# The FFN's output projection as seven Strassen products in chunks of K, on one Trainium2 core

## The chip, the cores and the metric

The program runs on one core of a Trainium2 chip. The metric is the device time of one execution in microseconds (us); the kernel before takes 2804.18 us (median of 3 runs, 2803.85 to 2805.12). Engines are named as in the profile: PE is TensorE (PEld its weight loads), DVE is VectorE, ACT is ScalarE, POOL is GpSimd, SP is the engine that issues all DMAs here.

## What is computed

A two-layer encoder on x of 1024 tokens by 1024 features, all in float32. Layer 0 mixes tokens by gated linear attention, layer 1 by differential attention. The change touches what follows the mixer in each layer:

```
h = h + mix
g, u = split(rms_norm(h, norm_ffn[i]) @ ffn_w_in[i])       # 1024 -> 2 x 2816
h = h + (silu(g) * u) @ ffn_w_out[i]                       # 2816 -> 1024: the output projection
gate = sigmoid(rms_norm(h, ple_norm[i]) @ ple_w_gate[i])   # 1024 -> 1024: the embedding gate
h = h + gate * (p[i] @ ple_w_proj[i])
```

## The kernel before

**Precision by three products.** Every float32 operand is split by `hi_lo` (line 119) into a rounded part (hi, a ScalarE copy to fp32r) and the rest (lo, a subtraction on VectorE, or on GpSimd where the call says so). `mm3` (line 154) then issues three matmuls, hi x lo, lo x hi and hi x hi (lines 156 to 158), into one PSUM accumulation. So a 128x128 by 128x512 block product costs three matmuls, one ScalarE copy per operand tile and one subtraction per operand tile.

**The FFN** is `ffn` (line 833 on), called once per layer. Its first part already uses seven Strassen products: K is 1024 (two halves of four blocks), and 22 units `u` (11 pairs `jp` of a gate unit and an up unit, 256 columns each) run seven products `(u, p)` each, of 12 matmuls. `prepare` splits weights five products ahead; `evac` adds the products in SBUF; in the up unit's `evac`, GpSimd multiplies into the tiles `sil` (L963), and one DMA per tile writes them to the scratch tensor `a_dram` (L964). The activations stand there transposed: 22 blocks of 128 features by 1024 tokens, even tokens' tiles and odd tokens' tiles side by side.

**The output projection** is the second part: `steps` is 2 halves of the tokens (s) by 22 blocks of K (j). `load_o` loads 128 rows of `ffn_w_out` (512 KB, tile `wr`) and, for each second block, 2 x 256 KB of activations (tile `ar`), four steps ahead. `split_o` splits both, two steps ahead. `out_step` issues 4 token tiles x 2 column halves x 3 matmuls = 24 matmuls into eight PSUM banks that stay open over all 22 blocks, and adds them to `out_h` (tiles `f0h`, reloaded by `load_h` from the scratch copy `h_mid`, four per half) at the half's end with VectorE (L1038).

```
for n in range(2):
    mm3(st["acc"][r][n], both(a, ALL, c), both(w, ALL, sl(n, 512)), j == 0, j == NJ - 1)
```

Beside it `next_pool`, which is `ple_weights`, loads and splits the embedding gate's weights (eight 512 KB tiles `pw_raw`, lo part on GpSimd, 128x1024 each) into a pool of its own. `early` prepares the first gate tile. Then class `Ple` runs the gates tile by tile, 48 matmuls each.

**What sets the order.** PE, DVE, ACT and POOL run their instructions in the order in which the program is written (`manual_schedule`). SP's order is set by the scheduler. All DMAs go out on one queue.

Of the kernel before, what the change touches and what calls it, by code (L numbers as in the profile page):

```python
# [18 lines left out]
P = 128  # L19
S = 1024  # L20
D = 1024
# [43 lines left out]
def kernel(  # L65
# [88 lines left out]
    def mm3(ps, lhs, rhs, start, stop):  # L154
        (lh, ll), (rh, rl) = lhs, rhs
        nc.tensor.matmul(ps, lh, rl, start=start, stop=False)  # L156
        nc.tensor.matmul(ps, ll, rh, start=False, stop=False)  # L157
        nc.tensor.matmul(ps, lh, rh, start=False, stop=stop)  # L158
# [671 lines left out]

    def ffn(layer, hs, tiles, g, hx_pools, bufs, next_pool, early):
# [3 lines left out]
        a_dram = dram.tile([NJ, P, 2, 512], F32, name=f"a_dram{layer}")  # L835
# [100 lines left out]
        def evac(u, p):  # L936
# [23 lines left out]
            else:  # L960
# [3 lines left out]
                nc.sync.dma_start(a_dram[2 * jp + i], sil)  # L964
# [27 lines left out]
        steps = [(s, j) for s in range(2) for j in range(NJ)]  # L992

        def load_o(q):
            s, j = steps[q]
            st["wr", q] = r = rawt(f"f{layer}_{q}wr")
            nc.sync.dma_start(r, w_out[sl(j), :])
            if j % 2 == 0:
                a = rawt(f"f{layer}_{q}ar", [2, 512])
                for i in range(2):  # L1000
                    nc.sync.dma_start(a[:, i, :].rearrange("p (h c) -> p h c", c=256), a_dram[j + i, :, :, sl(s, 256)])
                    st["ar", q + i] = a[:, i, :]

        def split_o(q):
            if q < 2:
                w = [pw.tile([P, D], F32R, tag="w", name=f"f{layer}_{q}wo{i}") for i in range(2)]
                a = pw.tile([P, 2, 512], F32R, tag="w", name=f"f{layer}_{q}ao")
                a = [a[:, i, :] for i in range(2)]
            else:
                if q == 2:  # L1010
                    st["W"] = [block_t(hx_pools[i % len(hx_pools)], f"f{layer}W{i}", bufs) for i in range(2)]
                    st["A"] = block_t(hx_pools[0], f"f{layer}A", bufs)
                i = q % 4
                w = [st["W"][i // 2][:, 2 * (i % 2) + z, :] for z in range(2)]
                a = [st["A"][:, i, sl(z, 512)] for z in range(2)]
            hi_lo(st.pop(("ar", q)), *a)
            hi_lo(st.pop(("wr", q)), *w)
            st["o", q] = (w, a)

        out_h = {}  # L1020
        ORDER = (2, 3, 0, 1)

        def out_step(q):
            s, j = steps[q]
            w, a = st.pop(("o", q))
            if j == 0:
                full = [ptA(f"f{layer}o{s}{i}") for i in range(2)]
                single = [[ptB(f"f{layer}o{s}{i}{n}") for n in range(2)] for i in (2, 3)]
                st["acc"] = [[full[i][:, n, :] for n in range(2)] for i in range(2)] + single
            for i, r in enumerate(ORDER):  # L1030
                if q == len(steps) - 1:
                    early(i, out_h)
                c = sl((r % 2) * 2 + r // 2)
                for n in range(2):
                    mm3(st["acc"][r][n], both(a, ALL, c), both(w, ALL, sl(n, 512)), j == 0, j == NJ - 1)
                for n in range(2 * (j == NJ - 1)):
                    h = out_h[4 * s + r][:, sl(n, 512)]
                    nc.vector.tensor_tensor(h, h, st["acc"][r][n], ALU.add)  # L1038

        def load_h(s):  # L1040
            for r in range(4):
                t = 4 * s + r
                out_h[t] = ht(f"f{layer}h{t}")
                nc.sync.dma_start(out_h[t], h_mid[sl(t), :])

        with tc.manual_schedule(engines={E.PE, E.DVE, E.Activation, E.Pool}):
# [32 lines left out]
            for z in seq:  # L1079
# [6 lines left out]
                else:  # L1086
                    while ready < min(n + (4 if n < 6 else 5), len(prods)):
                        prepare(ready)
                        ready += 1
                    if n == len(prods) - 3:  # L1090
                        for q in range(2):
                            load_o(q)
                        split_o(0)
                    prod(*z)
# [8 lines left out]
            mid.clear()  # L1103
            pool.release()
            later = next_pool()
            split_o(1)
            for q in range(2, 4):
                load_o(q)
            for q in range(len(steps)):
                if q + 2 < len(steps):  # L1110
                    split_o(q + 2)
                if q + 4 < len(steps):
                    load_o(q + 4)
                if 2 <= q < NJ - 4:
                    next(later, None)
                if q % NJ == NJ - 4:
                    load_h(q // NJ)
                if q == len(steps) - 2:
                    early(-1, out_h)
                out_step(q)  # L1120
# [3 lines left out]
    def ple_weights(layer):  # L1124
        pool = open_pool(f"plew{layer}")
        blk = [block_t(pool, f"pg{layer}{i}", 4) for i in range(4)]
        wgt = []

        def load():
            raw = {}  # L1130
            for i in range(KT + 1):
                if i < KT:
                    raw[i] = ht(f"pw{layer}{i}_raw")
                    nc.sync.dma_start(raw[i], ple_w_gate[layer][sl(i), :])
# [5 lines left out]
        return (pool, wgt), load()  # L1140

    class Ple:
# [38 lines left out]
        def nsq(self, t):  # L1181
            nm = f"nd{t}"
            junk = (pw if t == NT - 1 else praw).tile([P, D], F32, tag="w" if t == NT - 1 else "raw", name=nm + "sq")
            ss = tiny.tile([P, 1], F32, tag="ss", name=nm + "ss")
            nc.scalar.activation(junk, self.hs[t], AF.Square, accum_out=ss)
            self.st["nx", t] = self.hs[t] if 4 <= t < NT - 1 else junk, rstd_of(ss, 1, 1.0 / D, nm + "r")
# [4 lines left out]
        def ntr(self, t, hx):  # L1191
            transpose_t(self.st.pop(("nx", t))[0], *hx_t(hx, t), f"nd{t}")


    class Values:
# [16 lines left out]
        def blocks(self, hx, between):  # L1212
            for b in range(4):
                for half in range(2):
                    ps = ptA(f"dv{b}{half}").rearrange("p a (b f) -> p (a b) f", f=256)
                    for i in range(4):
# [11 lines left out]
                        if i < 3:  # L1228
# [3 lines left out]
                    nc.sync.dma_start(self.dram[half * 512:(half + 1) * 512, sl(b, 256)]  # L1232
                                      .rearrange("(k p) f -> p k f", p=P), v)
                    yield

    def diff(hx, hx_pools, h_dram, val, between):
# [387 lines left out]
    for layer in range(2):  # L1624
# [5 lines left out]
        def ple_pool():  # L1630
            (ple["pool"], wgt), gen = ple_weights(layer)
# [125 lines left out]
```

## Time and profile before

| | |
|---|---|
| time, median of 3 runs | 2804.18 us |
| the profiled execution: time, span | 2805.42 us, 2803.6 us |
| PE busy | 2742.5 us (98%) |
| POOL, DVE, ACT busy | 43%, 56%, 46% |
| first part of the FFN, layer 0 | 530 to 957 us of the span |
| output projection, layer 0 and layer 1 | 957 to 1198 us, 2465 to 2705 us |
| granted TensorE clock, mean | 0.998 |

Of an engine's row, busy time is the union of its instructions' spans; a matmul's span is longer than the distance to the next one, since matmuls are pipelined. A wait is read as the idle time before an instruction with what ended it.

### The profile page before, as it was taken

The page shows a single profiled execution, that of the slowest core. Times are in us where ns is not written, and L with a number is a line of the kernel's source. Part 1 is how long each engine was busy: PE and PEld are TensorE (multiplying, and loading weights), DVE is VectorE, ACT ScalarE, POOL GpSimd, SP SyncE. Part 2 cuts the span into 40 slices and gives each one's busy share as a digit, 9 for nine tenths or more (in the row PEclk, how much of TensorE's full clock was granted, in tenths as well). Part 3 has the DMA queues.
Part 4 walks back from the last instruction along what each step waited for, and adds up shares of the span by engine and source line. Part 5 has one row for each costly group of instructions (what it writes and reads, how often), then busy time and mean ns, then how long its engine had stood idle before and what let it go on. Part 6 is the DMA issues. An engine that isn't in the chain of part 4 may idle for free.

```text
span 2803.6 us, 40481 instructions
## 1 busy us (share of the span) xinstructions
PE 2742.5 (98%) x15272; PEld 2373.3 (85%) x15272; DVE 1571.3 (56%) x2390; ACT 1297.1 (46%) x2723; POOL 1204.1 (43%) x1364
## 2 busy tenths in 40 slices
PE   8999999999999999999999999989999999999999
PEld 7899988788888888889988999978878888888887
DVE  5677765654444534354258889886574444444333
ACT  5776663433333332233258878885343323342222
POOL 2243431365555420010578888873165555530000
PEclk9999999999999999999999999999999999999999
DMA  4122255222222564333221111136222222374422
GB/s 123 42 65 61 76 195 196 76 91 91 75 76 90 198 208 143 99 98 112 67 59 43 41 39 42 32 99 214 78 75 91 83 68 90 106 263 142 150 68 83
DMA packets 199956, 283.59 MB, mean 101 GB/s; under 512 B 14545, under 2 KB 158929, under 8 KB 199761
## 3 DMA queue, kind: packets, MB, share of 16 engines
q1 hardware_dynamic: 199760, 281.00, 31.2%
q8 instruction: 121, 1.98, 0.3%
q14 instruction: 75, 0.61, 0.1%
HBM read 215.95 MB, written 65.01 MB: 100 GB/s over the span
## 4 chain that ended last, share of the span: by engine, by line
PE 83%; DVE 7%; POOL 4%; ACT 3%; issue 2%; DMA 1%; SPq 0%; POOLq 0%; DVEq 0%; ACTq 0%
PE f1o L158 3%; PE f0o L156 3%; PE f0o L157 3%; PE f1o L156 3%; PE f1o L157 3%; PE f0o L158 3%; PE dp L156 2%; PE dp L158 2%; PE dp L157 2%; PE dv L156 1%; PE dv L158 1%; PE dv L157 1%; PE do L158 1%; PE do L156 1%; PE do L157 1%
## 5 line engine op out<-in xcount | busy, mean ns | idle before, releaser
L156 PE MATMUL dp<-dw,hxd 128*128 128x256 f32 x512 | 149.0, 291 | 2.0 <-DVE da17dt L1349 0.3
L158 PE MATMUL dp<-dw,hxd 128*128 128x256 f32 x512 | 144.9, 283 | 0.0
L157 PE MATMUL dp<-dw,hxd 128*128 128x256 f32 x512 | 144.7, 283 | 0.0
L156 PE MATMUL f1o<-f1W,f1A 128*128 128x512 f32 x336 | 130.8, 389 | 0.0
L156 PE MATMUL f0o<-f0W,f0A 128*128 128x512 f32 x336 | 130.8, 389 | 0.0
L158 PE MATMUL f0o<-f0W,f0A 128*128 128x512 f32 x336 | 130.7, 389 | 0.0
L158 PE MATMUL f1o<-f1W,f1A 128*128 128x512 f32 x336 | 130.7, 389 | 0.0
L157 PE MATMUL f0o<-f0W,f0A 128*128 128x512 f32 x336 | 130.7, 389 | 0.0
L157 PE MATMUL f1o<-f1W,f1A 128*128 128x512 f32 x336 | 130.7, 389 | 0.0
L156 PEld LDWEIGHTS dp<-dw,hxd 128*128 128x128 f32 x512 | 98.1, 192 | 3.5 <-DVE da17dt L1349 0.6
L157 PEld LDWEIGHTS dp<-dw,hxd 128*128 128x128 f32 x512 | 98.1, 192 | 0.1
L158 PEld LDWEIGHTS dp<-dw,hxd 128*128 128x128 f32 x512 | 97.9, 191 | 0.0
L158 PEld LDWEIGHTS f0o<-f0W,f0A 128*128 128x128 f32 x336 | 63.1, 188 | 13.2
L157 PEld LDWEIGHTS f1o<-f1W,f1A 128*128 128x128 f32 x336 | 63.1, 188 | 13.1
L158 PEld LDWEIGHTS f1o<-f1W,f1A 128*128 128x128 f32 x336 | 63.1, 188 | 13.1
L156 PEld LDWEIGHTS f0o<-f0W,f0A 128*128 128x128 f32 x336 | 63.1, 188 | 13.1
L156 PEld LDWEIGHTS f1o<-f1W,f1A 128*128 128x128 f32 x336 | 63.1, 188 | 12.9
L157 PEld LDWEIGHTS f0o<-f0W,f0A 128*128 128x128 f32 x336 | 63.1, 188 | 12.9
L156 PE MATMUL dv<-dwv,hxd 128*128 128x256 f32 x256 | 73.0, 285 | 0.0
L158 PE MATMUL dv<-dwv,hxd 128*128 128x256 f32 x256 | 72.4, 283 | 0.0
L157 PE MATMUL dv<-dwv,hxd 128*128 128x256 f32 x256 | 72.4, 283 | 0.0
L162 POOL TENSOR_SCALAR pn10r<-pn10ss 128x1 f32<-128x1 f32 x1 | 0.2, 191 | 166.3 <-ACT pn10xn L1152 166.3
(4446 smaller groups left out, 10008.0 us busy)
## 6 DMA issues: line engine op xcount, KB each, us to landing
pw_raw<-in_ple_w_gate_dram SPq DMA_DIRECT2D x16, 512.0 KB, 6.4
dqk_raw<-in_diff_w_in_dram SPq DMA_DIRECT2D x32, 256.0 KB, 3.7
x<-in_x_dram SPq DMA_DIRECT2D x8, 512.0 KB, 6.0
wv_raw<-in_gla_w_in_dram SPq DMA_DIRECT2D x8, 512.0 KB, 4.2
wr_raw<-in_gla_w_in_dram SPq DMA_DIRECT2D x8, 512.0 KB, 3.9
o_dram<-o SPq DMA_DIRECT2D x32, 128.0 KB, 1.8
r_dram<-r SPq DMA_DIRECT2D x16, 256.0 KB, 2.2
gwo_raw<-in_gla_w_out_dram SPq DMA_DIRECT2D x8, 512.0 KB, 3.6
```

The source lines that it names most:

```text
L156: nc.tensor.matmul(ps, lh, rl, start=start, stop=False)
L157: nc.tensor.matmul(ps, ll, rh, start=False, stop=False)
L158: nc.tensor.matmul(ps, lh, rh, start=False, stop=stop)
L162: nc.gpsimd.tensor_scalar(r, ss, scale, EPS, ALU.mult, ALU.add)
```

## The change

**The second product by Strassen as well.** K = 2816 is 22 blocks; blocks are paired into 11 pairs (`jp`): the even blocks are one half of K, the odd ones the other. Even and odd token tiles are the halves of the rows, columns 0 to 511 and 512 to 1023 the halves of the columns. For each pair there are seven left factors and seven right factors.

The left factors are made in the first part, by `sums_o`: after the up unit's multiplications GpSimd does four more 128x512 additions or subtractions per pair, and the seven factors (256 KB each) are written to `a_dram`, now `[8, 11, 128, 512]`. The right factors are made in the second part: `load_b` loads the rows of `ffn_w_out` once (tiles `b1` for even blocks, `b2` for odd ones), and `split_o` has GpSimd subtract 128x512 halves, four per pair, into tile `t` and back into `b1`; each subtraction is issued behind the split that reads the value before.

**Chunks.** The 11 pairs run in chunks of 4, 4 and 3; in a chunk the products come as 1, 5, 6, 3, 7, 2, 4 (in the last one 4 before 2), and each product runs over the chunk's pairs. That gives 28 + 28 + 21 = 77 steps of 12 matmuls (four token tiles x three), where 44 steps of 24 were. A PSUM group X (four banks) takes products 1, 6, 7, 4 one on top of the other, group Y takes 5, 3 and then 2. After a product's last step its running sum is added to four half tiles of `out_h`: after products 2, 3 and 4 by VectorE from PSUM; after 1, 5, 6 and 7 ScalarE copies PSUM to SBUF and GpSimd adds.

```diff
+        chunks = ((0, 4), (4, 4), (8, 3))
+        osteps = [(g, p, j) for g, (_, c) in enumerate(chunks)
+                  for p in ((1, 5, 6, 3, 7, 4, 2) if g == len(chunks) - 1 else (1, 5, 6, 3, 7, 2, 4)) for j in range(c)]
...
+        def load_ar(n):
+            g, p, j = osteps[n]
+            nc.sync.dma_start(half("ar", n % 4), a_dram[p, chunks[g][0] + j])
+
+        def split_o(n):
+            g, p, j = osteps[n]
+            b = lambda q: b_of(q, j)
+            sub = lambda dst, x, y: nc.gpsimd.tensor_tensor(dst, x, y, ALU.subtract)
+            st["o", n] = pair = [pw.tile([P, 2, 512], F32R, tag="w", name=f"f{layer}o{n}{z}") for z in "ab"]
+            for src, z in ((half("ar", n % 4), pair[0]), (b(p), pair[1])):
+                hi_lo(src, z[:, 0, :], z[:, 1, :])
+
+            if p == 1:
+                sub(b(5), b(7), b(1))
+            elif p == 5:
+                sub(b(6), b(3), b(5))
+            elif p == 6:
+                sub(b(4), b(2), b(6))
+            elif p == 3:
+                sub(b(7), b(3), b(7))
...
+            for r in range(4):
+                mm3(acc[r], (a[:, 0, sl(r)], a[:, 1, sl(r)]), (b[:, 0, :], b[:, 1, :]), j == 0 and p in (1, 5, 2), last,
+                    skip_group_check=True)
+            if not last:
+                return
+
+            for r in range(4):
+                h = {1: (1, 0), 2: (1, 0), 5: (0, 1), 7: (0, 1), 6: (1, 1), 3: (1, 1), 4: (0, 0)}[p]
+                h = out_h[2 * r + h[0]][:, sl(h[1], 512)]
+                if p in (2, 3, 4):
+                    nc.vector.tensor_tensor(h, h, acc[r], ALU.add)
+                else:
+                    st["u"] = u = (st.get("u", -1) + 1) % 8
+                    u = half(("t", "ar")[u // 4], 4 + u % 4)
+                    nc.scalar.copy(u, acc[r])
+                    nc.gpsimd.tensor_tensor(h, h, u, ALU.add)
...
             mid.clear()
+            load_h()
+            later = next_pool()
+            for n, (g, p, j) in enumerate(osteps):
+                if n + 4 < len(osteps):
+                    load_ar(n + 4)
+                if n + 2 < len(osteps):
+                    split_o(n + 2)
...
+                if n >= 8 and n % 4 == 0:
+                    next(later, None)
+                out_step(n)
```

Step n is PE's n-th group of 12 matmuls; its two operands (`a`, `b`) are split while step n-2 runs. The tiles of a split come from a pool of six, so a split can begin when PE has finished the step three before it. `load_ar` has four places. All eight tiles of `out_h` are loaded at once at the start of the second part.

**Even tiles first.** Product 4 ends the even token tiles before product 2 ends the odd ones, so the gates now run over tiles 0, 2, 4, 6, 1, 3, 5, 7 (`TILES`), and what reads their order downstream is renumbered (`PLACE`). The gate's weights go to the pools that the FFN's first part has left, their raw tiles to `praw`.

**How SP's order changes, layer 0.** The names: `f_10sil`, `f_10o` are pair 10's factors, `f0h` the tiles of `out_h`, `f0ar` the left factors' four places, `f0b` are `b1` and `b2`. Before, around the last writes of the first part:

```order
L1001 DMA f_2ar<-a_dram_5944 128x2x256 x2
L964 DMA a_dram_5944<-f_10sil_9495 128x1024
L997 DMA f_3wr<-in_ffn_w_out_dram 128x1024
L964 DMA a_dram_5944<-f_10sil_9496 128x1024
L997 DMA f_4wr<-in_ffn_w_out_dram 128x1024
L1001 DMA f_4ar<-a_dram_5944 128x2x256 x2
L997 DMA f_5wr<-in_ffn_w_out_dram 128x1024
L997 DMA f_6wr<-in_ffn_w_out_dram 128x1024
```

Now, at the same place:

```order
L975 DMA a_dram_5944<-f_10sil_9605 128x512
L1031 DMA f0ar<-a_dram_5944 128x512 x2
L975 DMA a_dram_5944<-f_10sil_9606 128x512 x2
L979 DMA a_dram_5944<-f_10o 128x512 x2
L979 DMA a_dram_5944<-f_10sil_9605 128x512
L979 DMA a_dram_5944<-f_10o_9771 128x512
L1080 DMA f0h_9783<-h_mid_5943 128x1024
...
L1080 DMA f0h_9797<-h_mid_5943 128x1024
L1031 DMA f0ar<-a_dram_5944 128x512 x4
L1183 DMA pw_raw<-in_ple_w_gate_dram 128x1024
```

Left factors 0 to 5 are issued ahead; those of steps 6 to 9 stand behind pair 10's seven writes and all eight `f0h` loads.

**POOL in the second part, layer 0.** Before, it had eight subtractions for the gate's weights and nothing else until the first gate tile:

```order
L963 TENSOR_TENSOR f_10sil_9495<-f_10sil_9495,f0cr 128x512 x2
L963 TENSOR_TENSOR f_10sil_9496<-f_10sil_9496,f0cr 128x512 x2
L121 TENSOR_TENSOR pg_9651<-pw_raw,pg_9650 128x1024 x4
L121 TENSOR_TENSOR pg_9653<-pw_raw,pg_9652 128x1024 x4
L162 TENSOR_SCALAR pn00r<-pn00ss 128x1
```

Now, the stretch of chunk 1 (steps 30 to 35 and what they release; L1036 makes right factors, L1075 adds to `out_h`):

```order
L1036 TENSOR_TENSOR f0t<-f0b_9680,f0t 128x512 x2
L1075 TENSOR_TENSOR f0h_9785<-f0h_9785,f0t 128x512
L1075 TENSOR_TENSOR f0h_9789<-f0h_9789,f0t 128x512
L1075 TENSOR_TENSOR f0h_9793<-f0h_9793,f0t 128x512
L1075 TENSOR_TENSOR f0h_9797<-f0h_9797,f0t 128x512
L1036 TENSOR_TENSOR f0t<-f0b_9680,f0t 128x512
L121 TENSOR_TENSOR pg_9802<-pw_raw,pg_9801 128x1024
L1036 TENSOR_TENSOR f0t<-f0b_9680,f0t 128x512 x3
L1075 TENSOR_TENSOR f0h_9783<-f0h_9783,f0ar 128x512
```

Per layer POOL's second part holds 44 right-factor subtractions and 48 additions (128x512) beside the eight gate subtractions (128x1024).

## Rows read from the trace of the kernel before

**Rows 1.** The page: busy time of the engines; a group of the costliest ones.
```profile
PE 2742.5 (98%) x15272; PEld 2373.3 (85%) x15272; DVE 1571.3 (56%) x2390; ACT 1297.1 (46%) x2723; POOL 1204.1 (43%) x1364
...
L156 PE MATMUL f0o<-f0W,f0A 128*128 128x512 f32 x336 | 130.8, 389 | 0.0
```

**Rows 2.** Tile f0o: duration ns min/median/max, first and last start.
```profile
L156 PE MATMUL f0o<-f_0wo,f_0ao x8: 389/389/389, 957.4 to 962.1; 128*128 128x512 f32 x8
```

**Rows 3.** Tile pl00g, the first gate.
```profile
L156 PE MATMUL pl00g<-pg,pn x16: 389/389/473, 1197.6 to 1208.8; 128*128 128x512 f32 x16
```

**Rows 4.** Windows: PE, PEld, DVE, ACT, POOL busy (instructions), PEclk, DMA share, GB/s.
```profile
530.00:957.40 427.40, 423.46 (x1858) 348.21 (x1857) 207.16 (x279) 139.53 (x243) 241.90 (x180) 1.00 0.27 90
957.40:1197.60 240.20, 240.20 (x1065) 199.01 (x1064) 97.09 (x105) 75.23 (x96) 26.22 (x14) 1.00 0.50 160
```

**Rows 5.** Groups by form in the output projection: busy, mean ns, idle before.
```profile
L121 DVE TENSOR_TENSOR f0A<-f_14ar,f0A 128x512 fp32r<-128x512 f32 x2 | 1.4, 692 | 6.5 <-ACT f0A L120 6.5
...
L120 ACT CAST f0A<-f_14ar 128x512 fp32r<-128x512 f32 x2 | 1.2, 624 | 7.7 <-PE f0o L158 7.7
```

**Rows 6.** Timeline of POOL in the first part, then at its end: start, length.
```profile
691.79 2.54 POOL L963 TENSOR_TENSOR f_3sil<-f_3sil,f0cr 128x512 f32<-128x512 f32 x2 [1.05 <-DVE f0cr L948]
694.29 1.30 POOL L121 TENSOR_TENSOR f_8w<-f_8s,f_8w 128x512 fp32r<-128x512 f32 x1
...
958.35 3.90 POOL L963 TENSOR_TENSOR f_10sil<-f_10sil,f0cr 128x512 f32<-128x512 f32 x2 [1.43 <-DVE f0cr L948]
973.23 2.49 POOL L121 TENSOR_TENSOR pg<-pw_raw,pg 128x1024 fp32r<-128x1024 f32 x1 [10.98 <-ACT pg L120]
```

**Rows 7.** Timeline of DVE where both DVE and POOL have work.
```profile
2050.71 1.77 DVE L121 TENSOR_TENSOR f1T<-nf17sq,f1T 128x512 fp32r<-128x512 f32 x1
2052.40 1.78 DVE L121 TENSOR_TENSOR f_0w<-f_0a,f_0w 128x512 fp32r<-128x512 f32 x1
2054.10 1.77 DVE L121 TENSOR_TENSOR f1T<-doh,f1T 128x512 fp32r<-128x512 f32 x1
2055.80 1.78 DVE L121 TENSOR_TENSOR f_1w<-f_1s,f_1w 128x512 fp32r<-128x512 f32 x1
2057.50 0.68 DVE L944 TENSOR_TENSOR f1cr<-f1cr,f_1ps 128x512 f32<-128x512 f32 x1
```

**Rows 8.** Timeline of POOL in the same stretch.
```profile
2053.59 1.74 POOL L917 TENSOR_TENSOR f_1a<-f_1a 128x512 f32<-128x512 f32 x1
2055.29 1.74 POOL L921 TENSOR_TENSOR f_1a<-f_1a,f_1s 128x512 f32<-128x512 f32 x1
2056.99 1.74 POOL L121 TENSOR_TENSOR f1T<-doh,f1T 128x512 fp32r<-128x512 f32 x1
```

**Rows 9.** Timeline of PE: the first part's product (8, 5).
```profile
701.93 0.39 PE L157 MATMUL f_8ps<-f0T,f_8w 128*128 128x512 f32 x1
```

**Rows 10.** Timeline of SP: the last write of the first part.
```profile
962.28 0.33 SPq L964 DMA_DIRECT2D a_dram<-f_10sil  x1
```

**Rows 11.** DMA issues: KB each, median us from issue to landing.
```profile
f0h<-h_mid SPq DMA_DIRECT2D x8, 512.0 KB, 4.3
...
f_0wr<-in_ffn_w_out_dram SPq DMA_DIRECT2D x2, 512.0 KB, 4.4
f_0ar<-a_dram SPq DMA_DIRECT2D x4, 256.0 KB, 3.2
```

**Rows 12.** Windows in two bursts of loads; columns as in Rows 4.
```profile
940.00:944.00 4.00, 4.00 (x19) 3.31 (x18) 0.69 (x1) 2.55 (x5) 2.34 (x2) 1.00 0.99 380
968.00:972.00 4.00, 4.00 (x19) 3.30 (x18) 2.52 (x3) 2.94 (x4) 0.00 (x0) 1.00 0.99 383
```

**Rows 13.** Windows around a wait of PE; columns as in Rows 4.
```profile
555.40:558.00 2.60, 0.57 (x2) 0.19 (x1) 2.11 (x3) 2.60 (x6) 2.60 (x3) 1.00 0.06 21
558.00:561.50 3.50, 3.50 (x8) 2.79 (x9) 2.78 (x3) 0.66 (x3) 3.33 (x2) 0.51 0.00 0
```

**Rows 14.** Timeline of PE in that second window.
```profile
559.43 0.63 PE L157 MATMUL f_0ps<-f0T,f_0w 128*128 128x512 f32 x1
559.86 0.63 PE L158 MATMUL f_0ps<-f0T,f_0w 128*128 128x512 f32 x1
```

More of the change, by code (lines that the diff above doesn't have):

```diff
@@ L989, in prepare @@
                 sums_a2(u)
[L992 to L1018, printed above, removed]
@@ L1020, in ffn @@
-        out_h = {}
[L1021 to L1038, printed above, removed]
@@ new lines, in out_step @@
+        def out_step(n):
+            g, p, j = osteps[n]
+            last = j == chunks[g][1] - 1
+            if j == 0 and p == 1:
+                st["X"] = [z[:, i, :] for z in [ptA(f"f{layer}o{g}x{i}") for i in range(2)] for i in range(2)]
+                st["Y"] = [ptB(f"f{layer}o{g}y{i}") for i in range(4)]
+            if j == 0 and p == 2 and g == len(chunks) - 1:
+                st["Y"] = [z[:, i, :] for z in [ptA(f"f{layer}o{g}z{i}") for i in range(2)] for i in range(2)]
+            acc = st["X" if p in (1, 6, 7, 4) else "Y"]
+            a, b = st.pop(("o", n))
+            for r in range(4):
+                mm3(acc[r], (a[:, 0, sl(r)], a[:, 1, sl(r)]), (b[:, 0, :], b[:, 1, :]), j == 0 and p in (1, 5, 2), last,
[12 more added lines that the diff above has]
+                    nc.gpsimd.tensor_tensor(h, h, u, ALU.add)
@@ L1043, in load_h @@
+        def load_h():
+            for t in range(NT):
                 out_h[t] = ht(f"f{layer}h{t}")
@@ L1103, in ffn, with ple_weights @@
             mid.clear()
-            pool.release()
[L1105 to L1120, printed above, removed]
+            load_h()
[5 more added lines that the diff above has]
+                    split_o(n + 2)
+                    if osteps[n + 2][1:] == (2, 0) and g + 1 < len(chunks):
+                        load_b(g + 1, 0)
+                    if osteps[n + 2][1:] == (4, 0) and g + 1 < len(chunks):
+                        load_b(g + 1, 1)
+                if n >= 8 and n % 4 == 0:
+                    next(later, None)
+                out_step(n)
+                if g == len(chunks) - 1 and (p, j) == (4, chunks[g][1] - 1):
+                    early(0, out_h)
+                if g == len(chunks) - 1 and (p, j) == (2, 1):
+                    early(1, out_h)
+            for _ in later:
+                pass
+            pool.release()
         return [out_h[t] for t in range(NT)]
-    def ple_weights(layer):
-        pool = open_pool(f"plew{layer}")
-        blk = [block_t(pool, f"pg{layer}{i}", 4) for i in range(4)]
+    TILES = (0, 2, 4, 6, 1, 3, 5, 7)
+    PLACE = {t: i for i, t in enumerate(TILES)}
+    def ple_weights(layer, pools, bufs):
+        blk = [block_t(pools[i % len(pools)], f"pg{layer}{i}", bufs) for i in range(4)]
         wgt = []
@@ L1139, in load @@
                 yield
-        return (pool, wgt), load()
+        return wgt, load()
     class Ple:
```

129 lines of the change are left out of this document (77 added, 52 removed).

## The prediction, made before the changed kernel was run

> **What bounds the kernel now.** I read the page first: PE is busy in 98% of the span [rows 1], so PE is the limit, and other engines matter where they make PE wait. The page gives 389 ns for a matmul of the output projection. That is a length, not a price, since matmuls overlap. So I read the stage itself: its first matmul starts at 957.4 us [rows 2], the first gate's at 1197.6 [rows 3]. In between stand 44 steps of 24 = 1056 matmuls: 240.2 / 1056 = **0.2275 us each**, with no idle time, since the window shows PE busy in all of its 240.2 us [rows 4]. The same window says how empty the other engines are there: DVE 97 us, ACT 75, POOL 26. In the first part of the FFN POOL is busy 242 of 427 us [rows 4].
>
> Then I looked for what new work would collide with. Where DVE and POOL both have a queue, subtractions that POOL does alone in 2.54 / 2 = 1.27 us [rows 6] and DVE in 0.69 [rows 5] come strictly in turn: DVE starts at 2050.71, 2052.40, 2054.10, 2055.80, POOL at 2053.59, 2055.29, 2056.99, both 1.70 apart [rows 7, 8]. So a pair, one of each, costs **1.70 us**, nearly the sum of the two. Only DVE's addition that reads PSUM takes its 0.68 beside a running POOL instruction [rows 7]. The reader is to see that for subtractions from SBUF the two engines are one resource.
>
> **What is removed.** Per layer 77 steps of 12 = 924 matmuls stand where 1056 were: 132 x 0.2275 = **-30.0 us** per layer. A step takes 12 x 0.2275 = 2.73 us of PE. By the 389 ns of the page it would be -51; the 0.2275 decides, since it is what the stage's end moves by.
>
> **What costs nothing.** ACT: two copies of 0.62 [rows 5] a step, 1.25 of 2.73, with bursts of four PSUM copies per product; a split runs two steps ahead, which covers it. DMA: some 40 MB in about 215 us, 190 GB/s against 380 in a burst [rows 12]; what it costs is the order, below. The four new POOL instructions per pair in the first part stand ahead of the split of the next unit's product 5. In the trace POOL is done with the multiplications at 694.33 and has 1.30 for that split [rows 6]: 694.33 + 4 x 1.27 + 1.30 = 700.7, with a DVE turn (0.43) in between 701.1; PE reads it at 701.93 [rows 9]. Hidden, with 0.8 to spare; if the cover is gone, every further DVE turn costs 0.43 at 10 places a layer. The order of the gates moves no work.
>
> **The load of `out_h`: a wait.** Count from PE's start of step 0. Before, POOL ended the last multiplication at 962.25 [rows 6], and SP issued the last write at 962.28 [rows 10], 4.9 us after that start. Now four subtractions follow on POOL, at 1.27 to 1.70 each, so the last of seven writes goes out at 10.0 to 11.7; I take 11. SP issues in order, so the eight loads of `out_h`, 512 KB each, come behind it, and the left factor of step 6 behind all eight. The first load lands 4.3 us after its issue [rows 11]; in a burst the queue moves 380 GB/s [rows 12], 1.37 us per load; 7 x 1.37 = 9.6, and 0.7 for the 256 KB of the factor. With 0.3 for issuing, 11 + 0.3 + 4.3 + 9.6 + 0.7 = 25.9; two ACT copies and the last DVE subtraction (0.62 + 0.62 + 0.69) give 27.8. PE is due at step 6 after 6 x 2.73 = 16.4. **+11.4 us** per layer. Bounds: 9 (POOL undisturbed, 3.2 us to the first landing as for the 256 KB loads), 13 (POOL always in turn, slower burst). POOL sits behind the same loads with its first additions, so what is late next is its queue.
>
> After such a wait PE's clock can be low: following a window in which PE was busy for 0.57 of 2.60 us the granted clock is 0.51 for 3.5 us, the 1.2 GHz level [rows 13], and matmuls start 0.43 us apart [rows 14]. Eight matmuls there cost 8 x (0.43 - 0.2275) = **+1.6 us**; ends 0 and, for two such stretches, 3.2.
>
> **DVE and POOL in turns: the largest unknown.** Each step needs two DVE subtractions. POOL gets 44 subtractions for right factors, 48 additions into `out_h` and the 8 long ones for the gates, 2.49 us each [rows 6], which is 1.2 more than a short one: a pair with a long one costs 2.90. As long as POOL has a backlog, two pairs = 3.40 us go by per step, and PE, which needs 2.73, is held to that. The backlog comes in a lump, since a chunk's sums for products 5, 6, 4 and 7 and the additions of products 1, 5 and 6 all fall between the ends of products 1 and 3:
> - chunk 1 (steps 28 to 55): 22 short and 3 long in a row = 22 x 1.70 + 3 x 2.90 = 46.1 us for 12.5 steps, for which PE needs 34.1. The splits are 1.1 us ahead when it begins: +10.9;
> - chunk 0: part of the backlog drains in the wait above; 14 short and 2 long = 29.6 for 8 steps, 21.8, lead 2.2: +5.6;
> - chunk 2 (three pairs): 19 short = 32.3 for 9.5 steps, 25.9, lead 1.8: +4.6.
>
> **+21.1 us** per layer. From below: if DVE always came first, PE would wait only for the chunk's last right factors, some 8.8 in chunk 1 (32.4 us of POOL and 14.3 of DVE in the 37.9 until the last is due) and 3 in the others: 12. From above: the pair costs the whole of both lengths, 1.30 + 0.69 = 1.99: the three lumps come to 10.2 + 18.1 + 10.1 = 38. I take 1.70, the one number of rows in which the same two shapes meet.
>
> The Trainium skill, SBUF — State Buffer, Who interferes with whom, says that a VectorE instruction with two SBUF inputs contends with GpSimd's reads, and that whoever issues first has the shared ports for the whole instruction. Taken by the profile's lengths that is the 1.99 and a time of about 2849; rows 7 and 8 show 1.70, so the measurement decides.
>
> **Chunk ends.** Group X of the next chunk (of product 2, in the last) waits for DVE's additions of product 4, which stand behind a split: the second of them (2 x 0.68) ends about 0.4 late, three times: **+1.2**; ends 0 and 2.
>
> **The sum** per layer: -30.0 + 11.4 + 1.6 + 21.1 + 1.2 = +5.3; two layers **+10.6**. The profiled execution took 2805.4 and would take 2816.0; it was 1.2 above the median of 2804.2, so I give **2815**.
>
> **Rivals.**
> 1. *The turns do not hold PE* (faster). The two-step lead of the splits absorbs them. It decides at two POOL instructions per step: with fewer, POOL has no backlog. The stage's total speaks for it: 154 DVE turns of about 0.55, 92 of 1.15 and 8 of 2.35 make 209 us, against 210 of PE, so spread evenly they would just fit; the lumps in POOL's order speak against it. Then 30.0 - 11.4 - 1.6 - 1.2 = 15.8 per layer: 2773.
> 2. *The loads do not hold PE.* The turns cost 21.1, but step 6 has its factor in time. The issue order speaks against it. 30.0 - 21.1 - 1.2 = 7.7: 2789.
> 3. *The clock falls again and again.* With a long subtraction, a step of PE waits up to 1.9 us (4.60 less 2.73), about the idle share that came before the 0.51 [rows 13]; 5 such steps a layer at 1.6 add 8.0: 2831. [...] Against it: PE stays busy for more than half of such a step.
> 4. *The whole gain*: neither wait, 2744.
> That the change does not do what it says I leave out: PE's order has 264 rows fewer, twice 132.
>
> **How the numbers follow.** My forecast, with its size open (h load 9 to 13, turns 12 to 38), has 0.57; rival 1 0.17, rival 2 0.09, rival 3 0.12, rival 4 0.05. About 0.2%, 5.6 us, is what a measurement tells from no change. Within the forecast most lies above 2809.8, some 0.16 within 2798.6 to 2809.8 and 0.04 below. Slower: 0.37 + 0.12 = 0.49; same: 0.16; faster: 0.04 + 0.17 + 0.09 + 0.05 = 0.35. The range 2770 to 2835 takes in rivals 1, 2 and 3 and leaves out rival 4, the half of rival 1's spread that lies below it, and the top of the forecast's bounds, together about 0.2. Slower cases alone would have 2800 to 2835.
>
> **What would show it.** Right: in the trace after, PE's output projection takes about 245 us per layer instead of 240.2; one idle stretch of some 11 us before step 6, ended by ScalarE or VectorE on `f0ar`, with the `f0h` loads landing just before; in chunk 1 PE waits of 0.7 us and more step after step, ended by VectorE, whose subtractions are 1.7 us long, and POOL without a gap; matmuls still 0.2275 apart otherwise. Wrong: no idle stretch before step 6 (the loads); VectorE's subtractions at 0.7 us, or POOL with gaps, in steps 32 to 44 (the turns); idle time in the first part of the FFN (POOL's four new instructions); many windows at 0.5 (rival 3).

## The result, and the profile after

The changed kernel takes **2836.25 us** (median of 4 runs, 2833.86 to 2836.55); the kernel before took 2804.65 in the same series. The ratio is 1.0111 (95% interval 1.0093 to 1.0128): slower by 31.6 us, where +10.6 was forecast. The profiled execution has a span of 2834.2 us, 30.6 more than before.

PE does less and waits more: its row of the page, against [rows 1], has 264 matmuls and 33 us less in it, and POOL has 432 us more. Below it stand two of POOL's new groups, its right factors and its additions into `out_h` (last column: the idle time before them and what ended most of it).

```profile
PE 2709.1 (96%) x15008; PEld 2323.8 (82%) x15008; DVE 1806.2 (64%) x2562; ACT 1383.5 (49%) x2951; POOL 1636.1 (58%) x1636
...
L1036 POOL TENSOR_TENSOR f0t<-f0b,f0t 128x512 f32<-128x512 f32 x22 | 34.2, 1562 | 26.1 <-DVE f0o59b L121 12.1
L1075 POOL TENSOR_TENSOR f0h<-f0h,f0ar 128x512 f32<-128x512 f32 x24 | 37.9, 1613 | 19.6 <-ACT f0ar L1074 19.6
```

The windows (columns as in [rows 4]) of layer 0: the whole output projection, the wait before step 6, step 6 itself, and step 28.

```profile
958.32:1212.79 254.47, 223.48 (x934) 174.52 (x932) 209.44 (x191) 120.01 (x211) 178.00 (x109) 0.97 0.44 141
972.60:987.80 15.20, 2.85 (x12) 2.02 (x13) 1.35 (x3) 2.00 (x4) 8.46 (x7) 0.72 0.96 364
987.80:993.05 5.25, 5.25 (x13) 4.12 (x13) 4.52 (x4) 1.22 (x3) 3.97 (x3) 0.51 0.60 155
1060.62:1064.90 4.28, 4.28 (x12) 3.38 (x13) 4.28 (x4) 0.00 (x0) 3.75 (x2) 0.60 0.15 25
```

The stage takes 254.5 us where it took 240.2 [rows 4]; in layer 1 253.9. A step that waits for nothing takes 2.72, so 77 of them would take 209.4: 30.8 are saved, and **45.1 are lost again**. The table puts down what each of the 77 steps lost over 2.72, from one step's start to the next one's:

| layer 0, us | forecast | measured |
|---|---|---|
| fewer matmuls | -30.0 | -30.8 |
| wait before step 6 (measured: 0.5 of it before step 5) | +11.4 | +13.2 |
| low clock: step 6; step 28 | +1.6; 0 | +2.5; +1.7 |
| turns: steps 11 to 18, 35 to 46, 62 to 71 | +5.6, +10.9, +4.6 | +6.9, +9.5, +4.6 |
| chunk ends: before steps 28, 56, 74 | +0.4 each | +2.7, +0.9, +0.9 |
| steps 22 and 23; the last two steps | 0 | +0.9; +1.3 |
| first part of the FFN, layer 0; layer 1 | 0 | +1.7; +1.2 |

**The wait before step 6.** SP's timeline (SPq is its queue): the last write of the first part at 970.17, 11.8 us after step 0's start (I had taken 11), all eight loads of `out_h` at once, and only then the factors of steps 6 to 9. PE's timeline shows the 12.35 us that follow, and the matmuls behind them, which start 0.42 us apart instead of 0.23: the granted clock is 0.51, the 1.2 GHz level.

```profile
970.17 0.32 SPq L979 DMA_DIRECT2D a_dram<-f_10o  x1
970.54 4.43 SPq L1080 DMA_DIRECT2D f0h<-h_mid  x8
975.07 5.24 SPq L1031 DMA_DIRECT2D f0ar<-a_dram  x4
```
```profile
987.80 0.79 PE L156 MATMUL f0o0y<-f0o6b,f0o6a 128*128 128x512 f32 x1 [12.35 <-DVE f0o6b L121]
...
988.82 0.63 PE L158 MATMUL f0o0y<-f0o6b,f0o6a 128*128 128x512 f32 x1
989.24 0.63 PE L156 MATMUL f0o0y<-f0o6b,f0o6a 128*128 128x512 f32 x1
```

**The turns, in chunk 1.** DVE's timeline, POOL's, PE's. DVE's subtractions start 1.70 apart, as in [rows 7]; the one that meets a gate's long subtraction takes 2.86; PE waits for DVE before each step, and from step 41 on it starts one each 3.40.

```profile
1097.80 1.77 DVE L121 TENSOR_TENSOR f0o41a<-f0ar,f0o41a 128x512 fp32r<-128x512 f32 x1
1099.50 2.86 DVE L121 TENSOR_TENSOR f0o41b<-f0b,f0o41b 128x512 fp32r<-128x512 f32 x1
1102.29 1.77 DVE L121 TENSOR_TENSOR f0o42a<-f0ar,f0o42a 128x512 fp32r<-128x512 f32 x1
1103.98 1.77 DVE L121 TENSOR_TENSOR f0o42b<-f0b,f0o42b 128x512 fp32r<-128x512 f32 x1
1105.68 1.78 DVE L121 TENSOR_TENSOR f0o43a<-f0ar,f0o43a 128x512 fp32r<-128x512 f32 x1
```
```profile
1097.29 1.74 POOL L1036 TENSOR_TENSOR f0t<-f0b,f0t 128x512 f32<-128x512 f32 x1
1098.99 2.83 POOL L121 TENSOR_TENSOR pg<-pw_raw,pg 128x1024 fp32r<-128x1024 f32 x1
1101.78 1.73 POOL L1036 TENSOR_TENSOR f0t<-f0b,f0t 128x512 f32<-128x512 f32 x1
1103.47 3.44 POOL L1036 TENSOR_TENSOR f0b<-f0b,f0b 128x512 f32<-128x512 f32 x2
```
```profile
1102.42 0.50 PE L156 MATMUL f0o1y<-f0o41b,f0o41a 128*128 128x512 f32 x1 [1.47 <-DVE f0o41b L121]
...
1105.81 0.50 PE L156 MATMUL f0o1y<-f0o42b,f0o42a 128*128 128x512 f32 x1 [0.33 <-DVE f0o42b L121]
```

**The end of chunk 0.** Product 4's last matmul starts at 1057.71. Its additions, which step 28 needs, are at 1059.20 on DVE. Six subtractions of steps 27 to 29 stand ahead of them, and four of these are drawn out, by a gate's weight and by the right factors of chunk 1, with which POOL begins just then. The ends of chunks 1 and 2 are another matter: there the additions come right behind DVE's splits, and PE waits 0.61 and 0.78 until the second of them is done.

```profile
1050.64 2.34 DVE L121 TENSOR_TENSOR f0o27a<-f0ar,f0o27a 128x512 fp32r<-128x512 f32 x1 [0.48 <-ACT f0o27a L120]
1052.90 1.78 DVE L121 TENSOR_TENSOR f0o27b<-f0t,f0o27b 128x512 fp32r<-128x512 f32 x1
1054.60 1.78 DVE L121 TENSOR_TENSOR f0o28a<-f0ar,f0o28a 128x512 fp32r<-128x512 f32 x1
1056.31 1.77 DVE L121 TENSOR_TENSOR f0o28b<-f0b,f0o28b 128x512 fp32r<-128x512 f32 x1
...
1059.20 2.47 DVE L1070 TENSOR_TENSOR f0h<-f0h,f0o0x 128x512 f32<-128x512 f32 x4
```
```profile
1049.43 3.00 POOL L121 TENSOR_TENSOR pg<-pw_raw,pg 128x1024 fp32r<-128x1024 f32 x1 [5.82 <-DMA f0ar<-a_dram]
1052.39 5.14 POOL L1036 TENSOR_TENSOR f0t<-f0b 128x512 f32<-128x512 f32 x3
```
```profile
1060.62 0.47 PE L156 MATMUL f0o1x<-f0o28b,f0o28a 128*128 128x512 f32 x1 [2.52 <-DVE f0h L1070]
...
1148.76 0.47 PE L156 MATMUL f0o2x<-f0o56b,f0o56a 128*128 128x512 f32 x1 [0.61 <-DVE f0h L1070]
```

**The first part, layer 1.** The four sums of pair 0 (L978) push POOL's split of unit 2's product 5 back to 2110.54, and PE waits 0.89 for it; unit 2 takes 20.00 us from the start of its first matmul to the start of its last, where it took 18.81.

```profile
2109.28 1.30 POOL L978 TENSOR_TENSOR f_0o<-f_0sil,f_0o 128x512 f32<-128x512 f32 x1
2110.54 1.72 POOL L121 TENSOR_TENSOR f_2w<-f_2s,f_2w 128x512 fp32r<-128x512 f32 x1
```
```profile
2112.32 0.50 PE L157 MATMUL f_2ps<-f1T,f_2w 128*128 128x512 f32 x1 [0.89 <-POOL f_2w L121]
```

In layer 0 of this profile unit 2 does not wait. PE was held up by 1.7 us in units 0 and 1, where the clock fell at 562.9 us, behind the wait shown here, and not at 558.1 as in the kernel before [rows 13]; so the split came in time.

```profile
562.19 0.47 PE L156 MATMUL f_0ps<-f0T,f_0w 128*128 128x512 f32 x1 [2.05 <-DVE f0T L121]
```

### The profile page after: what moved, and what is told of

Same layout as the page of the kernel before. It is cut to its first block, busy times and chain, and to the rows that moved or that the text cites. A ratio compares the mean times of both kernels' runs of the same rounds, so it can differ in the third digit from the quotient of the medians.

```text
span 2834.2 us, 41109 instructions
## 1 busy us (share of the span) xinstructions
PE 2709.1 (96%) x15008; PEld 2323.8 (82%) x15008; DVE 1806.2 (64%) x2562; ACT 1383.5 (49%) x2951; POOL 1636.1 (58%) x1636
## 4 chain that ended last, share of the span: by engine, by line
PE 70%; DVE 13%; POOL 8%; ACT 4%; issue 3%; DMA 2%; SPq 0%; ACTq 0%; DVEq 0%; POOLq 0%
PE dp L156 1%; PE dp L158 1%; PE dp L157 1%; PE dv L156 1%; PE dv L158 1%; PE dv L157 1%; PE do L156 1%; PE do L158 1%; PE do L157 1%; PE go L158 1%; PE go L156 1%; PE go L157 1%; POOL f1h L1075 0%; POOL f0h L1075 0%; DMA f1b<-in_ffn_w_out_dram 0%
## 5 line engine op out<-in xcount | busy, mean ns | idle before, releaser
L614 POOL TENSOR_TENSOR o<-o,gc 128x256 f32<-128x256 f32 x32 | 29.0, 906 | 98.3 <-ACT ob L608 90.1
L121 POOL TENSOR_TENSOR pg<-pw_raw,pg 128x1024 fp32r<-128x1024 f32 x16 | 44.8, 2798 | 17.2 <-ACT pg L120 11.4
L156 PE MATMUL do<-dwo,dot 128*128 128x512 f32 x128 | 50.8, 397 | 0.0
L156 PE MATMUL go<-gwo,got 128*128 128x512 f32 x128 | 50.7, 396 | 0.0
L120 ACT CAST pn<-pn_tp 128x512 fp32r<-128x512 f32 x32 | 17.2, 589 | 68.1 <-PE pn_tp L175 68.1
L158 PE MATMUL do<-dwo,dot 128*128 128x512 f32 x128 | 50.0, 390 | 0.0
L158 PE MATMUL go<-gwo,got 128*128 128x512 f32 x128 | 49.9, 390 | 0.0
L157 PE MATMUL go<-gwo,got 128*128 128x512 f32 x128 | 49.8, 389 | 0.0
L157 PE MATMUL do<-dwo,dot 128*128 128x512 f32 x128 | 49.8, 389 | 0.0
L1036 POOL TENSOR_TENSOR f0t<-f0b,f0t 128x512 f32<-128x512 f32 x22 | 34.2, 1562 | 26.1 <-DVE f0o59b L121 12.1
L1075 POOL TENSOR_TENSOR f0h<-f0h,f0ar 128x512 f32<-128x512 f32 x24 | 37.9, 1613 | 19.6 <-ACT f0ar L1074 19.6
L1075 POOL TENSOR_TENSOR f1h<-f1h,f1ar 128x512 f32<-128x512 f32 x24 | 37.9, 1612 | 19.5 <-ACT f1ar L1074 19.5
L157 PEld LDWEIGHTS dv<-dwv,hxd 128*128 128x128 f32 x256 | 49.1, 192 | 0.0
```

What stands on the lines that cost most here:

```text
L120: nc.scalar.copy(hi, src)
L121: (lo_eng or nc.vector).tensor_tensor(lo, src, f32(hi), ALU.subtract)
L156: nc.tensor.matmul(ps, lh, rl, start=start, stop=False, **kw)
L157: nc.tensor.matmul(ps, ll, rh, start=False, stop=False, **kw)
L158: nc.tensor.matmul(ps, lh, rh, start=False, stop=stop, **kw)
L614: nc.gpsimd.tensor_tensor(o, o, gcon["gout"], ALU.mult)
```

## The experiments

Ten kernels: runs 1 to 8 change the changed kernel, runs 9 and 10 change a run before them. My theory: the loss is the sum of the parts in the table, each with a mechanism of its own. The rival common to all: a part that is taken away only uncovers another wait. "Stage" is the output projection of layer 0, 254.5 us in the change; a ratio is to the kernel before, timed beside each.

**1. The loads of `out_h` spread out.**

```diff
         def load_h():
-            for t in range(NT):
-                out_h[t] = ht(f"f{layer}h{t}")
-                nc.sync.dma_start(out_h[t], h_mid[sl(t), :])
+            pass
...
                     load_ar(n + 4)
+                if n < NT:
+                    load_h1((1, 3, 5, 7, 0, 2, 4, 6)[n])
```

> The eight loads of out_h go out one per step (tiles 1, 3, 5, 7, 0, 2, 4, 6), each behind that step's left factor, so only two of them stand ahead of the factor of step 6; they still stand behind pair 10's seven writes. Theory (the burst of out_h loads makes step 6 wait): in the changed kernel those writes end 11.8 us after step 0's start; 11.8 + 0.3 + 4.3 to the first landing + 1.4 for the second tile + 0.7 for the factor + 2 for its split = 20.5, against 16.4 when PE is due: the wait falls from 13.1 to some 4 us, and the low clock behind it (2.5) to 0 or 1. Chunk 0 gives 2 to 4 back, since its backlog on GpSimd no longer drains in the wait. Some 8 us less per layer, 2820 (2812 to 2826). Rival (the wait is set by something else, GpSimd's sums or its additions): 2836.

2819.3, ratio 1.0046 (1.003 to 1.0063); stage 246.2. As the theory had it: step 6 waits 4.21 behind DVE instead of 12.35. The clock still falls behind that wait (step 6 takes 4.43), and chunk 0's turns now cost 7.3.

**2. And pair 10's writes behind the factors of steps 6 and 7.**

```diff
+                if jp == NG - 1:
+                    st.setdefault("late", []).append((p, z))
...
+                if n == 3:
+                    for q, z in st.pop("late"):
+                        nc.sync.dma_start(a_dram[q, NG - 1], z)
```

> As the run with the spread loads, and pair 10's seven writes now stand behind the factors of steps 6 and 7 instead of ahead of them. Theory (what makes step 6 wait is SP's order: writes that wait for GpSimd, then out_h): the factor of step 6 goes out at about 5 us after step 0's start and is split by 13, before PE is due at 16.4: no wait before step 6 and no low clock behind it. 13.1 + 2.5 less 2 to 4 that chunk 0 gives back: some 12.5 us less per layer, 2811 (2805 to 2818). Rival (something else holds step 6): 2836, or the same time as the run with the spread loads alone.

2820.2, ratio 1.0048 (1.0033 to 1.0063); stage 246.1: no better than run 1, so the rival of the series holds here. The wait before step 6 is gone, but POOL is then in turns with DVE from step 5 on, and every step from 5 to 16 takes 3.40: 8.2 us. DVE's timeline, with starts 1.70 apart, POOL's, and PE at step 18, which waits 3.79 behind DVE's additions of product 3 and a subtraction of 2.82, and runs at a granted clock of 0.50:

```profile
978.46 1.77 DVE L121 TENSOR_TENSOR f0o8a<-f0ar,f0o8a 128x512 fp32r<-128x512 f32 x1
980.15 1.78 DVE L121 TENSOR_TENSOR f0o8b<-f0t,f0o8b 128x512 fp32r<-128x512 f32 x1
981.86 1.78 DVE L121 TENSOR_TENSOR f0o9a<-f0ar,f0o9a 128x512 fp32r<-128x512 f32 x1
```
```profile
977.95 5.14 POOL L1081 TENSOR_TENSOR f0h<-f0h,f0t 128x512 f32<-128x512 f32 x3
983.05 6.85 POOL L1042 TENSOR_TENSOR f0t<-f0b,f0t 128x512 f32<-128x512 f32 x4
```
```profile
1019.38 0.80 PE L156 MATMUL f0o0x<-f0o18b,f0o18a 128*128 128x512 f32 x1 [3.79 <-DVE f0o18b L121]
```

In the change the window before step 6 has seven of these POOL instructions, next to DVE at work for only 1.35 of its 15.2 us: part of the turns was hidden under the long wait. Of the 8.4 us less in this stage 1.6 are step 28's low clock, which is absent here in layer 0; in layer 1 it is there, and 6.4 are gained.

**3. All seven products added by VectorE from PSUM.**

```diff
-                if p in (2, 3, 4):
+                if True:
                     nc.vector.tensor_tensor(h, h, acc[r], ALU.add)
```

> All seven products are added to out_h by VectorE from PSUM: 48 GpSimd additions and 48 ScalarE copies per layer are gone, 48 VectorE additions of 0.68 us (32.6 us) are new. Theory (VectorE and GpSimd in turns hold PE while GpSimd has a backlog): GpSimd keeps one subtraction per step at most beside the gates' long ones, a step then needs 1.70 + 0.69 = 2.4 of 2.73, and there is no backlog: of the stage's lost time the three lumps go (6.8 + 0.9, 9.4 and 4.45 = 21.5 us per layer), and with them most of what the chunk ends lose, 4 to 6 us; the wait before step 6 stays. 21.5 to 26 less per layer: 2790 (2782 to 2798). Rival (VectorE is simply short of time, whatever GpSimd does): VectorE has 32.6 us more work per layer, 2836 or slower.

2806.3, ratio 1.0001 (0.9992 to 1.0011); stage 239.1. VectorE has 48 instructions more and PE waits less: the rival (VectorE short of time) falls. The size is missed: 15.3 in layer 0, not 21.5 to 26. The lump of chunk 2 is gone, chunk 0's is down to 1.8; chunk 1 keeps 6.5 at steps 39 to 42, 1.7 of it at a granted clock of 0.62, where two gates' weights fall among the right factors. DVE's timeline shows a split that takes 2.89 beside one of them, PE's the waits.

```profile
1083.84 2.89 DVE L121 TENSOR_TENSOR f0o40a<-f0ar,f0o40a 128x512 fp32r<-128x512 f32 x1
```
```profile
1088.48 0.50 PE L156 MATMUL f0o1y<-f0o40b,f0o40a 128*128 128x512 f32 x1 [0.91 <-DVE f0o40b L121]
1091.88 0.50 PE L156 MATMUL f0o1y<-f0o41b,f0o41a 128*128 128x512 f32 x1 [0.36 <-DVE f0o41b L121]
1097.60 0.50 PE L156 MATMUL f0o1y<-f0o42b,f0o42a 128*128 128x512 f32 x1 [2.71 <-DVE f0o42b L121]
```

**4. PE kept busy in the wait.**

```diff
+            if n == 6:
+                pa, pb = st.pop("prev")
+                for i in range(48):
+                    nc.tensor.matmul(acc[i % 4], pa[:, 0, sl(i % 4)], pb[:, 0, :], start=False, stop=False,
+                                     skip_group_check=True)
```

> Ahead of step 6 PE runs 48 more matmuls on step 5's operands, 48 x 0.2267 = 10.9 us of the 12.35 that it waits there; so product 5 counts step 5 several times, and the sums are not the reference's. Theory (the step behind the wait is slow because PE stood idle and its clock fell): PE waits 1.5 us only, the granted clock stays at the upper level, step 6 takes 2.72 instead of 5.25: 2.5 less per layer, 2831 (2829 to 2833). Rival (step 6 is slow for another reason, its operands or the memory): 2836. Should the clock fall all the same, the 48 matmuls run past the wait and the time is above 2836.

2827.9, ratio 1.0076 (1.0061 to 1.0091); stage 249.6. Step 6 takes 2.85 at a granted clock of 1.00 instead of 5.25 at 0.51: the clock term is what the idle time costs. More came back than expected, part of it by chance: step 28 still waits 2.50 before it starts, yet in layer 0 it runs at 1.00 and takes 2.84 instead of 4.41, while in layer 1, behind the same 2.50, it runs at 0.62 and takes 4.34. Windows of step 6, of step 28, and of step 28 in layer 1:

```profile
988.48:991.33 2.85, 2.85 (x12) 2.36 (x13) 2.85 (x4) 1.22 (x3) 2.20 (x2) 1.00 0.56 186
...
1058.27:1061.20 2.93, 2.93 (x13) 2.42 (x14) 2.93 (x4) 0.00 (x0) 2.93 (x2) 1.00 0.04 15
...
2576.07:2580.41 4.34, 4.34 (x12) 3.46 (x13) 4.31 (x4) 0.00 (x0) 3.76 (x2) 0.62 0.18 51
```

**5. The gates' lo parts on VectorE.**

```diff
-                    hi_lo(raw.pop(k), *wgt[k], nc.gpsimd)
+                    hi_lo(raw.pop(k), *wgt[k])
```

> Only the lo parts of the gates' weights move from GpSimd to VectorE (eight 128x1024 subtractions per layer, 2.49 us each on GpSimd; on VectorE about 2 x 0.68). Theory (what costs is the turn, not GpSimd's length): GpSimd's lump of chunk 1 is 22 short subtractions instead of 22 and 3 long ones, but VectorE now has three more turns of its own in it, and those are longer (1.36 + 1.0): 19 x 1.70 + 3 x 2.37 = 39.4 us in which VectorE gets through 9.5 steps of splits, 25.9 us of PE; less the lead of 1.1 that is +12.4 where +10.9 was expected and 9.4 measured. No gain: 2836 (2831 to 2841). Rival (GpSimd's eight long instructions are what makes the lumps): 8 x 1.2 us per layer go, 2817.

2827.7, ratio 1.0079 (1.0064 to 1.0094); stage 249.3, 5.2 less (3.7 in layer 1): neither. The lumps stay as the turns would have it (6.2 in chunk 0 with a fall of the clock in it, 9.2, 4.6). What goes is in the main beside them: the wait at chunk 0's end falls from 2.52 to 1.37 and its low clock is gone (2.7 together), steps 22 and 23 lose nothing.

**6. Product 4 before product 2 in all chunks.**

```diff
-                  for p in ((1, 5, 6, 3, 7, 4, 2) if g == len(chunks) - 1 else (1, 5, 6, 3, 7, 2, 4)) for j in range(c)]
+                  for p in (1, 5, 6, 3, 7, 4, 2) for j in range(c)]
...
-                    if osteps[n + 2][1:] == (2, 0) and g + 1 < len(chunks):
+                    if osteps[n + 2][1:] == (4, 0) and g + 1 < len(chunks):
```

> Product 4 stands before product 2 in all three chunks, as in the last one, with the loads of the next chunk's rows moved to match; so group X is read out four steps before the next chunk writes it. Theory (the wait at a chunk's end is VectorE's additions of product 4, held up behind splits that go in turns with GpSimd): the 2.5 and 0.6 us before steps 28 and 56 go, and the low clock behind the first (1.7): 4.8 less per layer, 2826 (2823 to 2830); nothing else moves. Rival (step 28 waits for its own operands: the next chunk's rows, split late): 2836, with a wait of the same length ended by VectorE's split instead of its addition.

2829.6, ratio 1.0086 (1.0069 to 1.0103), an interval that still touches the change's; stage 250.9, 3.6 less. Steps 28 and 56 no longer wait for the additions, nor does the clock fall: the theory's mechanism. But a wait of 1.17 comes back before step 30, whose splits are now the late ones behind DVE's additions. Some 0.8 of the 3.6 are not the edit's: step 6 lost 1.8 at the low clock here, not 2.5.

**7 and 8. Runs 1 to 3 and 6 together; then run 5 as well.** Pair 10's writes stand behind the first four loads of `out_h` here (`n == 4`).

> Together: out_h's loads spread over the steps, pair 10's writes behind the first four of them, all seven products added by VectorE from PSUM, product 4 before 2 in every chunk; the gates' lo parts stay on GpSimd. Theory: no wait at step 6 (13.1 + 2.5), no lumps but for what the long subtractions leave (with the additions from PSUM alone 1.6 in chunk 0 and some 6 in chunk 1), no waits at the first two chunk ends; of the 44 us per layer that the stage loses some 10 stay: 2836 - 2 x 34 = 2768 (2758 to 2780). Rival (the waits only hide one another, as with the late writes, where the lump of chunk 0 took what the loads gave): half of it, 2800.

2785.5, ratio 0.993 (0.9915 to 0.9944); stage 231.0.

> The same, and the gates' lo parts on VectorE too, so that GpSimd has one short subtraction in four steps of seven and nothing else: no backlog anywhere. Theory: VectorE needs at most 1.70 + 0.69 + 0.68 of a step of 2.73 on average; of the 44 us per layer some 3 to 6 stay (the last chunk's end, the first gate tile): 2836 - 2 x 39 = 2758 (2750 to 2768), faster than the kernel before by 1.7 per cent. Rival (VectorE takes the lumps over, now that all sums are its own): 2770 to 2800.

**2764.6, ratio 0.9854 (0.9839 to 0.9868)**; stage 218.8, of which 209.4 is the matmuls. Run 7 came out slower than expected and run 8 as expected: moving the eight long subtractions off POOL, worth 5.2 us of the stage in run 5, is worth 12.2 here (11.2 in layer 1). Run 7's waits of 2.54 and 2.71 us before steps 14 and 42, each with a fall of the clock behind it, are 0.40 and 0.32 in run 8. The window of run 8's stage shows PE busy in 213.2 of 218.8, the clock at 1.00, POOL at 79 us:

```profile
956.54:1175.35 218.81, 213.19 (x934) 173.43 (x932) 186.36 (x247) 96.16 (x163) 79.28 (x53) 1.00 0.52 163
```

What it still loses: 2.6 around steps 5 and 6, 0.9 at each of four places where a product follows another in the same PSUM banks, and some 3 more in small pieces. One of the four, with the same wait of 0.61 as step 56 of the change:

```profile
1156.79 0.47 PE L156 MATMUL f0o2x<-f0o71b,f0o71a 128*128 128x512 f32 x1 [0.61 <-DVE f0h L1076]
```

**9. Run 8, with the sums of a pair behind the split for the next unit's product 5.**

```diff
-                if i == 1:
-                    sums_o(jp)
+                if i == 1 and jp == NG - 1:
+                    sums_o(jp)
+                elif i == 1:
+                    st["sums"] = jp
...
                         prepare(ready)
                         ready += 1
+                    if "sums" in st:
+                        sums_o(st.pop("sums"))
```

> As the run with everything, and in the first part of the FFN the four left-factor sums of a pair stand behind GpSimd's split for the next unit's product 5 instead of ahead of it. Theory (the first part got longer because that split, of unit 2, comes 3.5 us later than before the change and PE waits for it): the 0.9 us wait on the product-5 weights of unit 2 goes, 1.2 less per layer between unit 1 and unit 9; 2762.5 (2760 to 2765). Rival (unit 2 waits for the up unit's multiplications ahead of it, which did not move): 2764.6.

**2761.3, ratio 0.984 (0.9826 to 0.9853)**. The time alone could not tell this from run 8; the trace does. POOL's split of unit 2 comes straight after the multiplications, ahead of the sums (L986), and unit 2 of layer 1 takes 18.81 again, as in the kernel before. In layer 0 this profile has the late fall of the clock once more (at 561.7) and the first part is 1.7 longer than in the kernel before, although the sums no longer stand in the way; in run 10, where the fall is at 558.7, both layers are back to the first part's old length.

```profile
2064.21 5.95 POOL L965 TENSOR_TENSOR f_0sil<-f_0sil,f1cr 128x512 f32<-128x512 f32 x4
2070.11 1.76 POOL L121 TENSOR_TENSOR f_2w<-f_2s,f_2w 128x512 fp32r<-128x512 f32 x1
2071.83 1.28 POOL L986 TENSOR_TENSOR f_0o<-f_0sil,f_0sil 128x512 f32<-128x512 f32 x1
```

**10. Run 9, with the right factors on VectorE.**

```diff
-            sub = lambda dst, x, y: nc.gpsimd.tensor_tensor(dst, x, y, ALU.subtract)
+            sub = lambda dst, x, y: nc.vector.tensor_tensor(dst, x, y, ALU.subtract)
```

> As the run before it, and the 44 right-factor subtractions per layer go to VectorE, so that in the output projection GpSimd has nothing to do. Theory (a GpSimd subtraction costs VectorE a turn, about 1.0 us of delay, and a subtraction of VectorE's own costs 0.60): the small waits before steps 10, 14 and 42 (0.3 to 0.5 each) and the 0.5 at step 5 go; the 1.65 before step 6 and the four waits of 0.6 on the sums' PSUM groups stay: 1 to 1.7 less per layer than the run before, 2760 (2757 to 2763). Rival (VectorE becomes the bound where the sums and the right factors meet): slower than the run before by 2 to 6.

2762.2, ratio 0.9843 (0.983 to 0.9857); stage 218.6 against 219.2: no difference that the times can show. The waits at steps 10, 14 and 42 are gone; new ones stand at the start, 1.47 us in step 0 and 0.99 before step 4, where DVE's queue is full.

## Why the prediction was right and wrong

**Right: what bounds it, the side, and the two large terms.** A matmul is worth what the stage's end moves by: 30.8 against 30.0. Step 6 waits behind the burst of `out_h` loads; run 1 takes most of that wait away. And DVE and POOL in turns hold PE: in chunk 1 POOL works through the forecast's 22 short and 3 long instructions from 1073.94 to 1119.45 us, 45.5 for 46.1. Run 2 gives POOL a backlog earlier, and every step from 5 to 16 takes 3.40; run 3 takes most of the backlog away, and the lumps shrink or go. Rival 1 (the turns do not hold PE), rival 2 (the loads do not) and rival 4 fall with the table.

**Right in part by luck: the turns' total,** 21.1 forecast and 21.0 measured. Chunk 0 lost 1.3 more than forecast and chunk 1 1.4 less, and the two cancel; only chunk 2 came out by itself.

The Trainium skill, SBUF — State Buffer, Who interferes with whom, has the shared ports taken for a whole instruction. By the profile's lengths that made 1.99 a pair; the starts 1.70 apart in chunk 1 and in run 2 speak for the smaller price, as [rows 7, 8] did.

**Wrong: the size**, +5.3 forecast per layer, +16.0 and +14.9 measured. What failed are terms of the sum that were too small, and places that it put at nothing. Of the 10.7 missing in layer 0 the chunk ends make 3.3, the low clock 2.6, places not in the sum 2.2, the wait before step 6 1.8 and the first part 1.7; the matmuls give 0.8 back. The chunk ends (4.5) and the low clock (4.2) came out beyond the upper ends that were given for them, 2 and 3.2.

- *Chunk ends, 0.4 each*, measured 2.7, 0.9 and 0.9. I saw one split ahead of the additions and counted it at DVE's own length. At the end of chunk 0 the trace has six subtractions ahead of them, and the next chunk's right factors are on POOL by then, so that four go in turns or longer. I had counted POOL's backlog only between products 1 and 3. Run 6 shows that the additions are what step 28 waited for. At the other two ends the mechanism was right and its size was not: PE waits for the second addition, 0.9 instead of 0.4, and run 8 has the same 0.9 at four such places while POOL has little to do.
- *The low clock, 1.6*, measured 2.5 and 1.7. I carried over eight slow matmuls from [rows 13, 14]; step 6 ran whole at 0.51, 12 matmuls, and there was a second place, step 28, which the chunk end caused. Run 4 shows the term at step 6 to be one of idle time. Rival 3 (a fall at step after step) did not come: the waits of 1.47 and 1.64 at steps 41 and 46 left the clock up.
- *The wait before step 6, 11.4*, measured 13.2, just over the bound of 13. Of that 0.5 is lost before step 5 already, whose splits go in turns with POOL. The last write went out 0.8 later than the 11 that I chose within 10.0 to 11.7, and the burst was slower: by the landings in the trace the last of the eight loads comes 10.8 behind the first, not 9.6, while the first one lands 0.6 sooner than I had it.
- *"What costs nothing": the four new sums per pair.* I checked the cover at (8, 5), found 0.8 to spare, and took it for all pairs. At unit 2, where units 0 and 1 had been done out of the later pattern, it is gone: 1.2 us in layer 1, shown by run 9. The 1.7 of layer 0 is another thing, the late fall of the clock, and not the change's: with the same sums in the same place, runs 1 to 6 and 8 have the fall at 555.6 to 559.0 and unit 2's wait in layer 0 too, and there the first part is 1.2 longer. Why the fall comes early in one execution and late in another stays open.

Not in the sum at all were 0.9 at steps 22 and 23, where POOL's additions of product 7 and a gate's subtraction go in turns with DVE, and 1.3 at the last two steps, the first gate tile's transposes among them.

**Also missed:** I treated the terms as independent. They are not: in run 2 a wait of 13 and a low clock of 2.5 were taken away from the change's stage and only 8.4 came off it (6.4 in layer 1), since POOL works through its queue while PE waits. And the long gate subtractions are worth 5.2 us with the lumps and 12.2 without.

## What to carry to other kernels

When work moves from the engine that bounds a kernel to two others, count their turns stretch by stretch: where both have a queue of subtractions from SBUF, a pair costs nearly the sum. What VectorE reads from PSUM instead of SBUF stays out of these turns: four such additions in a row took 2.47 us with POOL at work and without. Here 48 additions per layer moved to VectorE, the busier of the two engines, and the stage became 15 us shorter. And when a wait is taken away, look first at what ran under it.

## What the runs showed that I had not expected

- The same wait with and without a fall of the clock: 2.52 us before step 28 in the change, then a granted clock of 0.60; 2.50 in run 4, then 1.00 in layer 0 and 0.62 in layer 1 of one execution. Its length alone does not tell what follows, so a gain of 1.6 us at such a place is not yet an edit's.
- A VectorE subtraction beside a 128x1024 GpSimd one took 2.82 to 2.89 us, as long as the GpSimd instruction itself; alone it takes 0.68.
- Runs 8 and 9 make the seven products pay: 2764.6 and 2761.3 against 2805.9 for the kernel before, with the same seven products as the change, in another order and on other engines.
